# Half of the last block's centring moved from VectorE to TensorE, as a float32 product with a diagonal matrix

## The chip, the cores and the metric

The kernel runs on one core of a Trainium2 chip. A core has TensorE (matrix products into PSUM), VectorE, ScalarE and GpSimd (elementwise work), and SyncE, which issues DMAs; GpSimd issues DMAs too. In the profile they are PE, DVE, ACT, POOL and SP. Each engine works through its own queue in order, and engines wait for each other by semaphores. The metric is the device time of one execution in microseconds (us); shorter is better.

## The reference

One layer of a streaming encoder over 1024 rows of 1024 columns, in float32. Six products of the input feed two branches (a gated linear recurrence and a multi-scale pooling), which are gated and merged; the merged rows go through `w_out`, are added to the input, and each row is normalized:

```python
y = jnp.einsum('bsd,de->bse', merged, w_out[l]) + b_out[l]
x = _layer_norm(DEEPNORM_ALPHA * x + y, ln_gain[l], ln_bias[l])

def _layer_norm(x, g, b):
    mu = jnp.mean(x, axis=-1, keepdims=True)
    var = jnp.mean(jnp.square(x - mu), axis=-1, keepdims=True)
    return (x - mu) * lax.rsqrt(var + LN_EPS) * g + b
```

The change concerns the last step alone: `(x - mu) * g`, then the division by the deviation, then `+ b`, for one block of 128 rows.

## The kernel before, in words

**Products.** Every large product is made of seven block products in place of eight (a Strassen scheme over 2 x 2 blocks), and every float32 operand is split into a rounded half (`h`) and a rest (`l`) of the type float32r, so that each product of 128x128 by 128x512 takes three passes: h by h, h by l, l by h. TensorE is busy nearly all the time.

**The end of the kernel.** The last product, merged by `w_out`, works on the rows in two halves: blocks 0 to 3 and blocks 4 to 7, of 128 rows each; tile `zt[s]` (in the profile `z`) holds block s, which starts as the biased input. `o_product` (line 1490) is 12 matmuls into a PSUM bank, and `o_add` (line 1449) adds a bank to half of the columns of a block. The loop over `O_STEPS` (line 1510) ends with blocks 0 to 3; the last loop (line 1534) makes blocks 4 to 7, each from two products: bank `oc`, subtracted from columns 512 to 1023, then bank `oe`, added to columns 0 to 511. For block 7 (`last`) the second product is made in two halves of 256 columns.

**The norm.** `o_norm(s)` (line 1463) follows. For blocks 0 to 6, VectorE makes the negative mean `nm` from sums that came with the additions, ScalarE squares the block (`sq`) with a running sum, and takes the root (`sd`); VectorE centres and multiplies by the scale in two halves (`y`), takes the reciprocal of `sd`, and ScalarE multiplies `y` by it. GpSimd then adds `y` to the rows of the output by a DMA that accumulates (`add_to`, line 672); the norm's bias had been written there before (line 1441). For block 7, VectorE takes the statistics of each 256 columns (`bn_stats`, `bn_aggr` into `mv`), ScalarE takes the root, VectorE centres and scales by the gain in two halves of 512 columns, takes the reciprocal, multiplies by it and adds the bias, again in two halves, and SyncE stores each half. `g_row` and `be_row` hold the gain and the bias on all partitions.

**What sets the order.** The code does not issue instructions; it adds tasks to a planner (`Plan`, line 162), which puts them in an order and then emits them. The planner steps through a time of its own with a cost for each task (lines 222 to 258): a GpSimd task takes 0.15 + 0.002 for each column, and is taken to be ready 0.1 later; a DMA from SP takes 0.07 and lands 1.9 later, and its bytes at 270 KB in a us more; a GpSimd DMA takes 1.05; a ScalarE copy 0.12 + 0.00083 for each column. When an engine is free, it starts, among the tasks whose operands are ready by that time, the one with the earliest due time. The due time is that of the tasks which use the result (what TensorE needs comes first), and 40 after TensorE's place in the program for tasks that nobody needs soon. TensorE and GpSimd are exceptions: their tasks keep the order of the program (line 217):

```python
t.chain = self.last.get(eng) if eng in ("PE", "POOL") or ... else None
```

On the chip, each engine then keeps the planned order, however late an operand comes.

Of the kernel before, what the change touches and what calls it, by code (L numbers as in the profile page):

```python
# [11 lines left out]
F32 = mybir.dt.float32  # L12
F32R = mybir.dt.float32r
AF = mybir.ActivationFunctionType
ALU = mybir.AluOpType

P = 128
S = 1024
# [390 lines left out]
def layer_kernel(ctx: ExitStack, tc: tile.TileContext, xq, x, w_in, par, wg, w_pool, wpa, wpb, w_out, rows, out):  # L409
    nc = Plan(tc)  # L410

    def pool(name, bufs, space=None):
        kw = {} if space is None else {"space": space}
        return Pool(ctx.enter_context(tc.tile_pool(name=name, bufs=bufs, **kw)), bufs, space is bass.MemoryType.DRAM)
# [9 lines left out]
    dram = pool("dram", 8, bass.MemoryType.DRAM)  # L424

    def xt(name, dt=F32R, shape=(P, 2, H)):
        return xpool.tile(list(shape), dt, tag="x", name=name)
# [7 lines left out]
    def kt(name, dt=F32):  # L435
        return kpool.tile([P, S], dt, tag="k", name=name)

    def et(name):
        return epool.tile([P, H], F32, tag="e", name=name)

    def bank(name):
        return psum.tile([P, H], F32, tag="ps", name=name)
# [4 lines left out]
    out = Ref(result, as_strided(Ref.base, [S, D], [D, 1]))  # L447
    HALF = [slice(0, H), slice(H, S)]
    V, A = nc.vector, nc.scalar
# [25 lines left out]
    KQ = 4  # L475
# [196 lines left out]
    def add_to(t, u):  # L672
        nc.gpsimd.dma_start(t, u, accum_op=ALU.add, max_dma_last_dim=2048)
# [174 lines left out]
    rcnt, ones = (const.tile([P, PAD], F32, name=n) for n in ("rcnt", "ones"))  # L848
# [63 lines left out]
    def b_pool(g):  # L912
# [15 lines left out]
        if g == 1:  # L928
# [5 lines left out]
    sp, m, nl, y, z, z2, acc = (const.tile([P, 8], F32, name=n)  # L934
                                for n in ("sp", "sp_m", "sp_nl", "sp_y", "sp_z", "sp_z2", "sp_acc"))
# [198 lines left out]
    g = Group("A0", w.out, X, *takes0)  # L1134
# [37 lines left out]
    due, pools, last, ends, W = {}, {}, [], [], {}  # L1172
# [6 lines left out]
    for i in range(1, len(order)):  # L1179
# [17 lines left out]
        if i > 1:  # L1197
            g = Group(f"{kind}{c}", W.pop(i), X, *takes)
# [124 lines left out]
    def o_sum4(p):  # L1323

        V.scalar_tensor_tensor(t2[p], t2[p], -1.0, sums[p, 1], ALU.mult, ALU.subtract)
# [43 lines left out]
    for i, (n, j) in enumerate(steps):  # L1369
# [7 lines left out]
        if j == 1:  # L1377
            a, c, m1, um = [[None] * KQ for _ in range(4)]
        X_, W_ = ([(hi_[:, k, :], lo_[:, k, :]) for hi_, lo_ in ops[i][o:o + 2] for k in range(2)] for o in (0, 2))
        for g in range(KQ):  # L1380
# [5 lines left out]
            for q in range(KQ):  # L1386
                sl = slice(q * P, (q + 1) * P)
# [43 lines left out]
    zt = {}  # L1431
# [3 lines left out]
    g_row, be_row = (xt(f"row{i}", F32, (P, S)) for i in (1, 2))  # L1435
# [3 lines left out]
    BY_DMA = (0, 1, 2, 3, 4, 5, 6)  # L1439
# [4 lines left out]
    nc.gpsimd.memset(eps, EPS)  # L1444
    stats = const.tile([P, 4, 6], F32, name="stats")
    last = NK - 1


    def o_add(s, e, ps, sign, first, final, sl=slice(0, H)):
        z = zt[s][:, e * H:(e + 1) * H][:, sl]  # L1450
        op = ALU.add if sign > 0 else ALU.subtract
        if final and s != last:
            V.scalar_tensor_tensor(z, z, ALPHA if first else 1.0, ps, ALU.mult, op, accum_out=acc[:, 2 * s + e:2 * s + e + 1])
        elif first:
            V.scalar_tensor_tensor(z, z, ALPHA, ps, ALU.mult, op)
        else:
            V.tensor_tensor(z, z, ps, op)
        if final and s == last:
            for k in (range(2) if sl == slice(0, H) else (sl.start // (H // 2),)):
                i = 2 * e + k  # L1460
                V.bn_stats(stats[:, i, :], zt[s][:, i * H // 2:(i + 1) * H // 2])

    def o_norm(s):
        sd = const.tile([P, 1], F32, name=f"sd{s}")
        sls = [slice(e * H, (e + 1) * H) for e in range(2)]
        if s == last:
            mv = const.tile([P, 2], F32, name=f"mv{s}")
            V.bn_aggr(mv, stats)
            A.activation(sd, mv[:, 1:2], AF.Sqrt, bias=eps)
            mean, op = mv[:, 0:1], ALU.subtract  # L1470
        else:
            nm, var = (const.tile([P, 1], F32, name=f"{n}{s}") for n in ("nm", "var"))
            V.tensor_scalar(nm, acc[:, 2 * s:2 * s + 1], acc[:, 2 * s + 1:2 * s + 2], -1.0 / D, ALU.add, ALU.mult)
            sq = kt(f"sq{s}")
            A.activation(sq, zt[s], AF.Square, bias=nm, accum_out=var)
            A.activation(sd, var, AF.Sqrt, bias=eps, scale=1.0 / D)
            mean, op = nm, ALU.add
        y = zt[s] if s == last else xt(f"y{s}", F32, (P, S))
        for sl in sls:
            V.scalar_tensor_tensor(y[:, sl], zt[s][:, sl], mean, g_row[:, sl], op, ALU.mult)  # L1480
        V.reciprocal(sd, sd)
        if s in BY_DMA:
            A.mul(y, y, sd)
            add_to(out[s * P:(s + 1) * P, :], y)
            return
        for sl in sls:
            V.scalar_tensor_tensor(y[:, sl], y[:, sl], sd, be_row[:, sl], ALU.mult, ALU.add)
            nc.sync.dma_start(out[s * P:(s + 1) * P, sl], y[:, sl])

    def o_product(ps, j, g, start, stop, sl=slice(0, H)):  # L1490
        for q in range(KQ):
            mh, ml = (t[:, q % 2, g * P:(g + 1) * P] for t in om[j][q // 2])
            wh, wl = (t[:, q % 2, sl] for t in ow[j][q // 2])
            for i, (l, r) in enumerate(((mh, wh), (mh, wl), (ml, wh))):
                nc.tensor.matmul(ps, l, r, start=start and q == 0 and i == 0, stop=stop and q == KQ - 1 and i == 2,
                                 skip_group_check=True)


    def operands(j):
        f, w = (xt, xt) if j == 2 else (kt, wt)  # L1500
        if j != 6:
            for p in range(2):
                load_wo(j, p, rt)
            for p in range(2):
                cast_wo(j, p, w)
        o_input(j, f)

    a, c = ([None] * KQ for _ in range(2))
    operands(6)
    for i, j in enumerate(O_STEPS[:5]):  # L1510
        if j == 6:
            for p in range(2):
                o_sum4(p)
        operands(O_STEPS[i + 2])
        for g in range(KQ):
            if j == 1:
                a[g] = bank(f"oa_{g}")
            elif j == 7:
                c[g] = bank(f"oc_{g}")
            ps = c[g] if j == 7 else a[g]  # L1520
            o_product(ps, j, g, j in (1, 7), j == 3)
            if j == 1:
                o_add(4 + g, 0, ps, 1, True, False)
            elif j == 6:
                o_add(4 + g, 1, ps, -1, True, False)
            elif j == 7:
                o_add(g, 1, ps, -1, True, False)
            elif j == 5:
                o_add(g, 1, ps, -1, False, True)
            else:  # L1530
                o_add(g, 0, ps, 1, True, True)
                o_norm(g)

    for g in range(KQ):
        o_product(c[g], 4, g, False, True)
        o_add(4 + g, 1, c[g], -1, False, True)
        pieces = (slice(0, H),) if g < KQ - 1 else (slice(0, H // 2), slice(H // 2, H))
        for sl in pieces:
            ps = bank(f"oe_{g}_{sl.start}")[:, 0:sl.stop - sl.start]
            o_product(ps, 2, g, True, True, sl)  # L1540
            o_add(4 + g, 0, ps, 1, False, True, sl)
        o_norm(4 + g)
    nc.emit()

# [53 lines left out]
```

## Time and profile before

| | us |
|---|---|
| median of 3 runs | 739.97 |
| lowest and highest of them | 739.44, 1909.23 |
| the profiled execution | 739.99 |
| span of the profiled execution | 738.2 |
| its TensorE, busy | 730.1 |
| last matmul of `oe` begins | 730.64 |
| first and second store of block 7 issued | 734.47, 735.13 |

The span runs from the first to the last instruction that the profiler saw; the time of an execution is 1.8 us longer. In the views, a row of the timeline has the start in us from the span's start, the length in us, the engine, the line (that of the planner's helper for all: L396), the operation, output<-inputs by the tiles' names, their shapes, and in brackets how long the engine had been idle and what ended that. DMA queue q0 holds what GpSimd issues, q1 what SyncE issues; "us to landing" is the time from the issue of a DMA until its completion is seen.

### The profile page before, as it was taken

What the parts mean: (1) busy time and instruction counts of PE and PEld (TensorE: products, weight loads), DVE (VectorE), ACT (ScalarE), POOL (GpSimd) and SP (SyncE); (2) the same over time, 40 slices, a digit from 0 to 9 for tenths busy, and PEclk for the clock granted to TensorE, in tenths of its full rate; (3) what the DMA queues carried; (4) which work ended last, traced back from release to release, by engine and by line L of the source; (5) the groups of instructions that cost most, each with busy time, mean ns of one, the idle gap of its engine ahead of it and who ended that gap; (6) DMA issues with size and microseconds to landing.
All of it is one profiled execution on the core that took longest, in us unless ns stands there. A gap on an engine that the chain in (4) does not pass through costs nothing.

```text
span 738.2 us, 8796 instructions
## 1 busy us (share of the span) xinstructions
PE 730.1 (99%) x3254; PEld 599.4 (81%) x3254; DVE 600.5 (81%) x741; ACT 459.6 (62%) x588; POOL 69.7 (9%) x119
## 2 busy tenths in 40 slices
PE   9999999999999999999999999999999999999996
PEld 7887888888887878788888888888888888888885
DVE  6998896969696878977986768879948886999676
ACT  6686969686877868688844445447553545325473
POOL 0071111111001111100011000100000000000021
PEclk9999999999999999999999999999999999999999
DMA  8247888678988989750386954999679996758757
GB/s 317 86 158 200 282 180 267 142 240 214 306 167 217 327 210 279 203 126 35 110 201 127 235 121 158 275 293 346 230 259 302 314 328 232 245 224 229 199 84 145
DMA packets 64227, 158.98 MB, mean 215 GB/s; under 512 B 4340, under 2 KB 8308, under 8 KB 64120
## 3 DMA queue, kind: packets, MB, share of 16 engines
q1 hardware_dynamic: 43784, 106.39, 41.6%
q0 software_dynamic: 20112, 51.91, 33.7%
q8 instruction: 25, 0.41, 0.2%
q10 hardware_dynamic: 288, 0.13, 0.1%
q14 instruction: 18, 0.15, 0.1%
HBM read 137.43 MB, written 77.07 MB: 291 GB/s over the span
## 4 chain that ended last, share of the span: by engine, by line
PE 99%; DVE 0%; DVEq 0%; issue 0%
PE a_A L396 11%; PE a_B L396 11%; PE a_G L396 11%; PE oa L396 6%; PE pa_b L396 6%; PE pa_a L396 6%; PE c_B L396 6%; PE c_A L396 6%; PE c_G L396 5%; PE ps_s L396 3%; PE oc L396 3%; PE pc_b L396 3%; PE pc_a L396 3%; PE ps_pool L396 3%; PE e_B L396 3%; PE e_A L396 3%
## 5 line engine op out<-in xcount | busy, mean ns | idle before, releaser
L396 ACT ACT_TABLE_LOAD x38 | 48.8, 1283 | 2.4 <-PEq L1590 1.6
L396 DVE SCALAR_TENSOR_TENSOR xc<-xp,par_sb,xc 128x1023 f32<-128x1023 f32 (+2 forms) x24 | 30.7, 1280 | 0.5
L396 DVE TENSOR_TENSOR i<-i,xc 128x1024 f32<-128x1024 f32 x8 | 9.8, 1224 | 25.5 <-ACT i L396 25.5
L396 PE MATMUL pa_a<-oh,oh 128*128 128x512 f32 x64 | 24.9, 389 | 0.0
L396 PE MATMUL pa_a<-ol,oh 128*128 128x512 f32 x64 | 24.9, 389 | 0.0
L396 PE MATMUL pa_a<-oh,ol 128*128 128x512 f32 x64 | 24.9, 389 | 0.0
L396 PE MATMUL pa_b<-oh,oh 128*128 128x512 f32 x64 | 24.9, 389 | 0.0
L396 PE MATMUL pa_b<-ol,oh 128*128 128x512 f32 x64 | 24.9, 389 | 0.0
L396 PE MATMUL pa_b<-oh,ol 128*128 128x512 f32 x64 | 24.9, 389 | 0.0
L396 ACT ACTIVATE zb<-zb,par_sb 128x1024 f32<-128x1024 f32 (+1 forms) x16 | 15.0, 939 | 13.3 <-DVE zb L396 13.2
L396 ACT ACTIVATE r<-ps_g,par_sb 64x512 f32<-64x512 f32 x32 | 21.9, 685 | 2.1 <-DVE rb_B L396 0.8
L396 ACT ACTIVATE i<-ps_g,par_sb 64x512 f32<-64x512 f32 x32 | 21.9, 685 | 1.9 <-DVE r L396 1.4
L396 PE MATMUL c_A<-x64h,wd_A 128*128 128x512 f32 x64 | 21.0, 389 | 0.0
L396 PE MATMUL c_B<-x64h,wd_B 128*128 128x512 f32 x64 | 21.0, 389 | 0.0
L396 POOL DMA_DIRECT2D out<-y x7 | 8.5, 1210 | 130.5 <-ACT sd L396 117.6
L396 PE MATMUL ps_pool<-mixh,wp 128*128 128x512 f32 x64 | 20.4, 389 | 0.0
L396 PE MATMUL e_A<-x,wah_A 128*128 128x512 f32 x64 | 19.7, 389 | 0.0
L396 PE MATMUL e_B<-x,wah_B 128*128 128x512 f32 x64 | 19.7, 389 | 0.0
L396 POOL COPY paced<-pace 128x1 f32<-128x1 f32 x17 | 6.8, 399 | 124.6 <-ACT pace L396 124.6
L396 PE MATMUL c_G<-x64h,wd_G 128*128 128x512 f32 x56 | 18.4, 389 | 0.0
L396 DVE TENSOR_TENSOR_SCAN r<-a,i 128x1024 f32<-128x1024 f32 x8 | 18.3, 2282 | 0.1
L396 PE MATMUL e_G<-x,wah_G 128*128 128x512 f32 x56 | 17.2, 389 | 0.0
(521 smaller groups left out, 2537.4 us busy)
## 6 DMA issues: line engine op xcount, KB each, us to landing
sg<-sg SPq DMA_DIRECT2D x16, 512.0 KB, 4.7
ra_A<-in_w_in SPq DMA_DIRECT2D x8, 512.0 KB, 7.0
rb_A<-in_w_in SPq DMA_DIRECT2D x8, 512.0 KB, 6.5
xb<-bias SPq DMA_DIRECT2D x4, 1024.0 KB, 11.6
ya<-r SPq DMA_DIRECT2D x8, 512.0 KB, 6.1
xb<-in_x POOLq DMA_DIRECT2D x4, 1024.0 KB, 9.8
ra_B<-in_w_in SPq DMA_DIRECT2D x8, 512.0 KB, 5.4
rb_B<-in_w_in SPq DMA_DIRECT2D x8, 512.0 KB, 6.2
```

The lines of the kernel that those rows point to most:

```text
L396: getattr(getattr(nc, t.op[0]), t.op[1])(*a, **k)
```

## The change

For block 7, columns 512 to 1023 (`two`) are no longer centred on VectorE. With g the gain, (x - mu) * g = x * g - mu * g. GpSimd makes x * g (`zg`), and TensorE adds two float32 products in one PSUM bank, `centred`: an identity matrix times `zg`, and a diagonal matrix with -mu of each row times the gain. Columns 0 to 511 (`one`) are centred on VectorE as before. The scaling then reads the first half from SBUF and the second from the bank.

The tile `eye` (128x512) holds three 128x128 matrices beside each other: ONE is the identity, MINUS its negative, DIAG the diagonal with -mu. ONE is made through DRAM: GpSimd clears the tile; SyncE writes 128x129 zeros of it to `eye_d`, writes 128 ones to the first column there, and reads the first 128 * 128 numbers back as rows of 128, so that the ones lie on the diagonal. ScalarE makes MINUS once, and DIAG from it when the mean is known, ahead of the root. All this stands in the program between the loop over `O_STEPS` and the last loop.

The stores of blocks 0 to 6 are now put on a list and issued by `stores.pop()()`: for blocks 0 to 3 at the same place as before, for blocks 4 to 6 in the next turn of the last loop, behind its first `o_add`; in the last turn `zg` stands ahead of block 6's store.

```diff
     stats = const.tile([P, 4, 6], F32, name="stats")
     last = NK - 1
+    stores = []
...
         if s == last:
             mv = const.tile([P, 2], F32, name=f"mv{s}")
             V.bn_aggr(mv, stats)
+            mean, op = mv[:, 0:1], ALU.subtract
+            one, two = sls
+            y = zt[s]
+            V.scalar_tensor_tensor(y[:, one], y[:, one], mean, g_row[:, one], op, ALU.mult)
+            A.mul(eye[:, DIAG], eye[:, MINUS], mean)
             A.activation(sd, mv[:, 1:2], AF.Sqrt, bias=eps)
-            mean, op = mv[:, 0:1], ALU.subtract
+            nc.tensor.matmul(centred, eye[:, DIAG], g_row[:, two], start=False, stop=True, skip_group_check=True)
+            V.reciprocal(sd, sd)
+            for sl, src_ in ((one, y[:, one]), (two, centred)):
+                V.scalar_tensor_tensor(y[:, sl], src_, sd, be_row[:, sl], ALU.mult, ALU.add)
+                nc.sync.dma_start(out[s * P:(s + 1) * P, sl], y[:, sl])
+            return
...
-        y = zt[s] if s == last else xt(f"y{s}", F32, (P, S))
+        y = xt(f"y{s}", F32, (P, S))
         for sl in sls:
             V.scalar_tensor_tensor(y[:, sl], zt[s][:, sl], mean, g_row[:, sl], op, ALU.mult)
         V.reciprocal(sd, sd)
-        if s in BY_DMA:
-            A.mul(y, y, sd)
-            add_to(out[s * P:(s + 1) * P, :], y)
-            return
-        for sl in sls:
-            V.scalar_tensor_tensor(y[:, sl], y[:, sl], sd, be_row[:, sl], ALU.mult, ALU.add)
-            nc.sync.dma_start(out[s * P:(s + 1) * P, sl], y[:, sl])
+        A.mul(y, y, sd)
+        stores.append(lambda: add_to(out[s * P:(s + 1) * P, :], y))
...
                 o_norm(g)
+                stores.pop()()
+
+    ONE, MINUS, DIAG = (slice(i * P, (i + 1) * P) for i in range(3))
+    eye, zg = et("eye"), et("zg")
+    eye_d = dram.tile([P, P + 1], F32, tag="eye", name="eye_d")
+    nc.gpsimd.memset(eye, 0.0)
+    nc.sync.dma_start(eye_d, eye[:, 0:P + 1])
+    nc.sync.dma_start(eye_d[:, 0:1], ones[:, 0:1])
+    nc.sync.dma_start(eye[:, ONE], eye_d.rearrange("a b -> (a b)")[0:P * P].rearrange("(p m) -> p m", m=P))
+    A.mul(eye[:, MINUS], eye[:, ONE], -1.0)
 
     for g in range(KQ):
         o_product(c[g], 4, g, False, True)
         o_add(4 + g, 1, c[g], -1, False, True)
+        if g == KQ - 1:
+            nc.gpsimd.tensor_tensor(zg, zt[last][:, HALF[1]], g_row[:, HALF[1]], ALU.mult)
+        if g:
+            stores.pop()()
         pieces = (slice(0, H),) if g < KQ - 1 else (slice(0, H // 2), slice(H // 2, H))
         for sl in pieces:
             ps = bank(f"oe_{g}_{sl.start}")[:, 0:sl.stop - sl.start]
             o_product(ps, 2, g, True, True, sl)
             o_add(4 + g, 0, ps, 1, False, True, sl)
+        if g == KQ - 1:
+            centred = bank("centred")
+            nc.tensor.matmul(centred, eye[:, ONE], zg, start=True, stop=False, skip_group_check=True)
         o_norm(4 + g)
     nc.emit()
```

## The prediction

> **What bounds the kernel now.** I read the page first, for the engine that carries the span, then the chain of waits over the last 40 us.
>
> ```profile
> PE 730.1 (99%) x3254; PEld 599.4 (81%) x3254; DVE 600.5 (81%) x741; ACT 459.6 (62%) x588; POOL 69.7 (9%) x119
> ...
> PE 99%; DVE 0%; DVEq 0%; issue 0%
> ```
>
> TensorE is the bound until its last product. The chain's last pieces (start, length, what):
>
> ```profile
> 722.61 2.72 PE oe L396 x12
> ...
> 728.05 2.88 PE oe L396 x24
> 730.93 0.02 issue
> 730.95 0.43 DVE z L396
> ...
> 731.41 0.44 DVE stats L396
> ...
> 731.87 0.27 DVE mv L396
> ...
> 732.17 1.42 DVE z L396 x2
> 733.58 0.09 DVE sd L396
> ...
> 733.69 0.75 DVE z L396
> 734.44 0.66 DVEq L1594
> ```
>
> From 730.95 on, VectorE alone carries the end: the last addition, the statistics, two centrings (1.42 us together where one takes 0.75, so the second costs some 0.66), the reciprocal, two scalings. Only this tail can get shorter; even all of its 4 us is 0.6% of the run. The other rows that matter are of block 6 and block 7 on VectorE, then on ScalarE:
>
> ```profile
> 728.01 0.16 DVE L396 RECIPROCAL sd<-sd 128x1 f32<-128x1 f32 x1 [0.25 <-ACT sd L396]
> 728.09 0.68 DVE L396 TENSOR_TENSOR z<-z,oc 128x512 f32<-128x512 f32 x1
> ...
> 729.97 0.43 DVE L396 BATCH_NORM_STATS2 stats<-z 128x6 f32<-128x256 f32 x1
> 730.95 0.42 DVE L396 TENSOR_TENSOR z<-z,oe 128x256 f32<-128x256 f32 x1 [0.55 <-PE oe L396]
> ```
>
> ```profile
> 722.77 1.15 ACT L396 ACTIVATE y<-y,sd 128x1024 f32<-128x1024 f32 x1 [0.23 <-DVE sd L396]
> 726.40 1.16 ACT L396 ACTIVATE sq<-z,nm 128x1024 f32<-128x1024 f32 x1 [2.48 <-DVE nm L396]
> ...
> 728.21 1.15 ACT L396 ACTIVATE y<-y,sd 128x1024 f32<-128x1024 f32 x1 [0.23 <-DVE sd L396]
> 732.17 0.29 ACT L396 ACTIVATE sd<-mv,eps 128x1 f32<-128x1 f32 x1 [2.81 <-DVE mv L396]
> ```
>
> The reciprocal of block 6 stands in VectorE's queue ahead of all of block 7 and waits for ScalarE; VectorE's only slack behind it is the 0.55 us before 730.95. So what holds ScalarE up before 726.40 by more than 0.55 us moves the end.
>
> **The gain meant.** One centring leaves VectorE: the first scaling starts where the second centring did, and the last store is issued 0.66 us sooner, if nothing else is late. Two things must be there in time. The reciprocal needs `sd`, which now stands behind the 128x128 scaling that makes DIAG (nearest row, ScalarE's 128x128 cast, 297 ns, below): 732.17 + 0.30 + 0.29 = 732.76, and the one centring ends about 732.83, so no wait. The second scaling needs `centred`: DIAG at 732.47, VectorE free for it at about 732.17 + 0.66 + 0.09 + 0.66 = 733.6, so the float32 product has 1.1 us. No float32 product stands in the trace. From below it is one pass, 2.72 / 12 = 0.23; the nearest row for full accuracy is this kernel's own split in three passes, 0.68; from above a whole group of twelve, 2.72, a wait of 1.6 that would turn the gain into a loss of 0.9. I take 0.68: no wait. The Trainium skill, FP8 and Floating Point Precision, section TensorE Precision Notes, speaks against it: true float32 costs four passes through the array. By that rule it is 0.91 us, still inside the 1.1, and the sum stays; no run here shows it. The other product (eye times zg) runs while VectorE takes the statistics.
>
> **What the change adds to the queues.** GpSimd's order is the program's. So the clearing of `eye` stands behind block 3's store, and zg between the stores of blocks 5 and 6.
>
> ```profile
> 716.86 1.21 POOL L396 DMA_DIRECT2D out<-y  x1 [1.74 <-ACT y L396]
> ...
> 724.32 1.20 POOL L396 DMA_DIRECT2D out<-y  x1 [3.49 <-ACT y L396]
> 729.72 1.21 POOL L396 DMA_DIRECT2D out<-y  x1 [4.20 <-ACT y L396]
> ```
>
> ```profile
> L396 POOL TENSOR_TENSOR sp_acc<-sp_acc,sp_z 128x8 f32<-128x8 f32 x9 | 5.1, 567 | 0.8
> ...
> L396 POOL MEMSET rcnt<- 128x1 f32 x16 | 0.6, 103 | 0.0
> ...
> L396 POOL MEMSET ones<- 128x16 f32 x1 | 0.1, 112 | 0.3 <-POOLq L1590 0.3
> ```
>
> ```profile
> L396 ACT CAST gh<-gr 128x128 fp32r<-128x128 f32 x8 | 2.4, 297 | 0.0
> ```
>
> Clearing: 9 ns more for 15 more columns, so 0.1 + 0.3 for 512; done at 718.07 + 0.4 = 718.5. zg: at least 0.57 (the 128x8 row); two VectorE passes, 1.5, is my upper end; I take 1.1. Then come three DMAs on SP, each waiting for the one before: 66 KB out, 128 single numbers out, 64 KB back. SP has nothing else to issue until the last stores, so nothing is queued behind them there; but ScalarE's MINUS waits for the third. What such a DMA takes, free and beside GpSimd's traffic:
>
> ```profile
> gr<-in_wg SPq DMA_DIRECT2D x1, 64.0 KB, 1.8
> ```
>
> ```profile
> DMA packets 346, 0.81 MB, mean 238 GB/s; under 512 B 12, under 2 KB 12, under 8 KB 346
> ## 3 DMA queue, kind: packets, MB, share of 16 engines
> q0 software_dynamic: 346, 0.81, 109.9%
> issues: line engine op xcount, KB each, median us to landing
> rb_B<-in_w_in SPq DMA_DIRECT2D x1, 512.0 KB, 6.9
> gr<-in_wg SPq DMA_DIRECT2D x1, 64.0 KB, 8.1
> ```
>
> The first is the stretch 41.5 to 42.5, with idle queues: 1.8 us. The second is 287.3 to 290.7, with GpSimd's queue full: SP's two loads had been issued, and in 3.4 us not one packet of theirs moved (only q0 has a row). And this is the stretch in which `eye` is made, 718.5 to 725.5:
>
> ```profile
> DMA  9999999998999999999999999999989989999952
> ...
> q0 software_dynamic: 704, 1.35, 108.5%
> ```
>
> It is full, until about 725.5. Bounds for each DMA: 1.8 and 8.1 us. A free SP transfer moves its first packet 0.8 us after issue (the last stores, below), so a full queue costs 3.4 - 0.8 = 2.6 more, and I take 4.4 for the first: 722.9. The second would meet the same, but the queue runs empty at about 725.6; it lands 1.0 later, 726.6. The third is free: 728.4.
>
> **Where ScalarE waits.** Where MINUS stands in ScalarE's queue is the planner's choice, by its own figures (they order, they are no times of the chip). In its list for the kernel before, block 3's store starts at 716.36, and block 5's scaling `y` can start at 725.15. The clearing follows at 716.36 + 1.05, and by the planner's formulas MINUS is ready 1.27 + 2.21 + 1.97 + 2.21 later, at 725.08, when ScalarE is free: MINUS goes just ahead of block 5's `y`. On the chip that `y` started at 722.77. It, and block 6's square, now stand behind a wait that ends at 728.4.
>
> The sum: MINUS to 728.7, `y` of block 5 1.05 more, so the square of block 6 at 729.8 instead of 726.40, 3.4 late. Block 6's reciprocal, and VectorE behind it, is 3.4 late; 0.55 of slack goes; the tail starts 2.85 late. Less the 0.66 gained, the stores are issued 2.2 late.
>
> ```profile
> 734.47 1.02 SPq L396 DMA_DIRECT2D out<-z  x2
> ```
>
> ```profile
> DMA  8350000003999999999999993000000000000000
> ...
> out<-z SPq DMA_DIRECT2D x2, 256.0 KB, 2.1
> ```
>
> ```profile
> out<-y POOLq DMA_DIRECT2D x1, 512.0 KB, 5.5
> ```
>
> Before, GpSimd's last store (issued 729.72, 5.5 to landing) moved its last packets at about 734.7 (the strip runs from 734.4, 0.095 us a digit), and the last two stores had the queues alone from 735.3 to 736.7; the second landed at 735.1 + 2.1 = 737.2, and the span ended 1.0 later. Now block 5's store leaves at 724.32 + 5.95 = 730.3; block 6's `y` is 3.4 late, zg ends at 732.2 + 1.1 = 733.3, and block 6's store leaves then, behind block 5's: its packets run to about 738.6, over the last two stores, issued at 736.6 and 737.3. Free they land at 739.4; wholly behind, 738.6 + 1.4 + 0.5 = 740.5. The middle, 740.0, is 2.8 after 737.2. The profiled execution took 739.99 (its span 738.2, and 1.8 around it; the median is 739.97), so **742.8**, and 742.2 to 743.4 for the two ends.
>
> **Rivals.** *The change does what it says* (`eye` by 725.0: three free DMAs give 718.5 + 5.5 = 724.0, and a `y` that is 1.5 us late reaches nobody). Then 0.66 less; zg still pushes block 6's store by 0.3, whose packets then run into the last two stores' for some 0.3: 739.6. For it: 1.8 us free. Against it: the full strip.
>
> *SP's packets get their turns.* With 59.8 us of packet time (109.9% of 16 engines over 3.4 us) a packet of q0 takes 0.17 us; 8 rows an engine would wait 8 x 0.17 = 1.4, so 3.2 for a DMA: 721.7, 724.9, and `eye` at about 726.9. The tail is then 1.35 late, less 0.66, plus 0.4 of mixing: 741.1. The Trainium skill, DMA: Bandwidth & Descriptors, section Queues, rings and completion order, has this rule: each engine goes round its queues by packets. The 3.4 us without a packet speak against it here.
>
> *Later still, plainly slower.* If MINUS falls behind block 5's `y` (0.07 decides in the plan), that store leaves on time, and its packets fill the queue for the third DMA: 726.6 + 4.4 = 731.0. The square of block 6 starts at 731.3, 4.9 late; 4.9 - 0.55 - 0.66 = 3.7, with 0.5 of mixing: 744.2. The second DMA, of single numbers, can bring the same by being slower than any row shows. To reach 2% (14.8 us) all three would have to take 8.1.
>
> **Numbers.** Forecast 0.50; as meant 0.17; turns 0.15; later 0.13; 0.05 for something else (the product as the last wait among it, about 740.5). The range 739.6 to 745.0 leaves out some of the gains and of the latest cases. What a measurement of this kernel can tell is about 2%; every case but the 8.1 one is within it: faster 0.01, same 0.98, slower 0.01.
>
> **What would show it.** Right: the trace after has MINUS on ScalarE between block 5's `sd` and `y`, idle until a DMA into `eye` at about 728; a reciprocal of block 6 that waits for `sd` some 3 us; one centring of 128x512 at the end, and a scaling from `centred` that doesn't wait. Wrong: `eye` there before 725.5 (the DMAs weren't held), `y` of block 5 at 722.8 (the order was another), or a wait for `centred`.

## The result and the profile after

| | before | after |
|---|---|---|
| median, us | 739.9 | 743.77 (742.74 to 744.44, 6 runs) |
| ratio of the times | | 1.0052, 95% interval 1.0042 to 1.0063 |
| the profiled execution | 739.99 | 743.75 |
| its span | 738.2 | 742.0 |
| `mv` of block 7 known | 732.13 | 735.00 |
| second store of block 7 issued | 735.13 | 738.37 |

The change costs 3.9 us, half a per cent: reliably more than nothing, and far within 2%. One of the six executions before took 1909.23 us, and the ratio leaves it out. The forecast was 742.8 with a range from 739.6 to 745.0.

ScalarE's timeline after the change, at the place where MINUS was expected:

```profile
721.86 0.29 ACT L396 ACTIVATE sd<-var,eps 128x1 f32<-128x1 f32 x1
728.77 0.31 ACT L396 ACTIVATE eye<-eye 128x128 f32<-128x128 f32 x1 [6.61 <-DMA eye<-eye_d]
728.98 1.14 ACT L396 ACTIVATE y<-y,sd 128x1024 f32<-128x1024 f32 x1
730.02 1.13 ACT L396 ACTIVATE sq<-z,nm 128x1024 f32<-128x1024 f32 x1
...
735.04 0.40 ACT L396 ACTIVATE eye<-eye,mv 128x128 f32<-128x128 f32 x1 [2.09 <-DVE mv L396]
```

MINUS stands between `sd` and `y` of block 5 and idles ScalarE for 6.61 us; the square of block 6 starts at 730.02 (726.40 before). What it does to VectorE:

```profile
731.61 0.16 DVE L396 RECIPROCAL sd<-sd 128x1 f32<-128x1 f32 x1 [4.22 <-ACT sd L396]
731.69 0.67 DVE L396 TENSOR_TENSOR z<-z,oc 128x512 f32<-128x512 f32 x1
...
734.74 0.26 DVE L396 BATCH_NORM_AGGREGATE mv<-stats 128x2 f32<-128x24 f32 x1
735.04 0.75 DVE L396 SCALAR_TENSOR_TENSOR z<-z,mv,row 128x512 f32<-128x512 f32 x1
735.71 0.15 DVE L396 RECIPROCAL sd<-sd 128x1 f32<-128x1 f32 x1
735.90 0.75 DVE L396 SCALAR_TENSOR_TENSOR z<-z,sd,row 128x512 f32<-128x512 f32 x1
737.59 0.75 DVE L396 SCALAR_TENSOR_TENSOR z<-centred,sd,row 128x512 f32<-128x512 f32 x1 [0.94 <-PE centred L396]
```

The reciprocal of block 6 comes 3.60 later than before, and all of block 7 behind it. One centring is left, as meant; the second scaling waits 0.94 for the product, which it was not to do. TensorE shows why, in its timeline and then in three stretches (the columns of the second are length, busy time of PE, PEld, DVE, ACT and POOL, granted clock, DMA share, GB/s):

```profile
730.26 0.28 PE L396 MATMUL oe<-wo2h,o2l 128*128 128x256 f32 x1
733.77 2.03 PE L396 MATMUL centred<-zg,eye 128*128 128x512 f32 x2 [3.23 <-POOL zg L396]
735.59 1.90 PE L396 MATMUL centred<-row,eye 128*128 128x512 f32 x2
```

```profile
728.00:731.00 3.00, 2.54 (x22) 2.33 (x20) 0.00 (x0) 2.23 (x3) 0.48 (x1) 1.00 0.07 19
731.00:734.00 3.00, 0.23 (x1) 0.24 (x2) 2.32 (x7) 1.69 (x4) 2.25 (x3) 0.97 0.62 70
734.00:737.30 3.30, 3.30 (x4) 0.72 (x4) 2.51 (x6) 0.58 (x2) 0.87 (x1) 0.51 1.10 178
```

A float32 product is two matmuls. TensorE had stood without work for 3.23 us, its granted clock is 0.51 in the last stretch, and there the product on the path takes 1.90 us. GpSimd's queue and the transfers into `eye`:

```profile
717.08 1.19 POOL L396 DMA_DIRECT2D out<-y  x1 [1.76 <-ACT y L396]
717.80 1.01 POOL L396 MEMSET eye<- 128x512 f32 x1
...
730.52 1.18 POOL L396 DMA_DIRECT2D out<-y  x1 [9.49 <-ACT y L396]
732.45 1.26 POOL L396 TENSOR_TENSOR zg<-z,row 128x512 f32<-128x512 f32 x1 [0.75 <-DVE z L396]
733.67 1.21 POOL L396 DMA_DIRECT2D out<-y  x1
```

```profile
eye_d<-eye SPq DMA_DIRECT2D x1, 64.5 KB, 5.6
eye<-eye_d SPq DMA_DIRECT2D x1, 64.0 KB, 1.7
eye_d<-ones SPq DMA_DIRECT2D x1, 0.5 KB, 2.6
```

The transfers follow each other from 718.84 to 728.66. The page sums its chain of waits over the whole span, so TensorE's products before the end hide this; the same chain, cut to the end of the span, shows where its last stretch starts (start, length, what):

```profile
687.66 10.00 DMA wor<-in_w_out
...
704.33 1.25 ACT sq L396 x2
...
717.80 1.01 POOL eye L396
...
721.03 9.47 issue
...
732.45 1.27 POOL zg L396
...
733.77 3.73 PE centred L396 x4
```

It begins with a load of `w_out` that lands at 697.66 and runs through the norms of blocks 0 to 3 to the clearing. From there it stays in GpSimd's queue; its 9.47 of "issue" is the time in which block 5's store waits for ScalarE's `y` (GpSimd's rows above), which stands behind MINUS and so behind `eye`. In the kernel before, the chain is TensorE's products up to 730.93, and none of this set the end.

The 3.74 us that the span grew are, from these rows: `mv` later by 2.87; from `mv` to the issue of the second store 3.37 instead of 3.00, so +0.37; from there to the end of SP's wait for the landing (740.63, before 737.19) 2.26 instead of 2.06, so +0.20; and from there to the end 1.33 instead of 1.03, so +0.30.

### The profile page after: what moved, and what is told of

Read it like the earlier page. It is cut to its first block, busy times and chain, and to the rows that moved or that the text cites. A ratio compares the mean times of both kernels' runs of the same rounds, so it can differ in the third digit from the quotient of the medians.

```text
span 742.0 us, 8817 instructions
## 1 busy us (share of the span) xinstructions
PE 733.5 (99%) x3258; PEld 601.1 (81%) x3258; DVE 599.8 (81%) x740; ACT 459.9 (62%) x590; POOL 71.2 (10%) x121
## 4 chain that ended last, share of the span: by engine, by line
PE 93%; issue 2%; ACT 2%; DMA 1%; DVE 1%; POOL 1%; POOLq 0%; ACTq 0%; DVEq 0%
PE a_A L396 11%; PE a_B L396 11%; PE a_G L396 10%; PE pa_b L396 6%; PE pa_a L396 6%; PE c_B L396 6%; PE c_A L396 6%; PE c_G L396 5%; PE ps_s L396 3%; PE oa L396 3%; PE pc_b L396 3%; PE pc_a L396 3%; PE ps_pool L396 3%; PE e_B L396 3%; PE e_A L396 3%; PE e_G L396 3%
```

## The experiments

Each is compared with the kernel before on the same chip (739.83 in the first group of four, 739.66 in the second of four, 739.49 in the last of three).

**The transfers early.** The eight lines that make `eye` are put ahead of the loop over `O_STEPS`; `nc.not_until(698.0)` keeps the planner from starting them before that time of its own.

```diff
+    with nc.not_until(698.0):
+        ONE, MINUS, DIAG = (slice(i * P, (i + 1) * P) for i in range(3))
...
+        A.mul(eye[:, MINUS], eye[:, ONE], -1.0)
     a, c = ([None] * KQ for _ in range(2))
```

> The changed kernel, with the making of `eye` (clearing, three DMAs, MINUS) moved ahead of the first output product, when GpSimd stores nothing yet. Theory (the loss is ScalarE's wait for `eye`): block 6's square starts at about 726.4 again, the mean of block 7 is known at about 732.1, 2.9 us sooner than in the changed kernel; the wait for `centred` of some 0.9 us stays, so that the second store leaves about 0.4 later than in the kernel before: 740.3 us. Rival (the float32 products, zg and the moved stores cost the time): it stays above 742.5. Second rival (without the hold the gain is as meant): 739.3.

740.17 us, ratio 1.0003 (0.9994 to 1.0012). The 3.9 us are gone, and the 0.66 that the change was to bring doesn't show either. Its timelines on VectorE and TensorE:

```profile
732.58 0.75 DVE L396 SCALAR_TENSOR_TENSOR z<-z,sd,row 128x512 f32<-128x512 f32 x1
733.40 0.75 DVE L396 SCALAR_TENSOR_TENSOR z<-centred,sd,row 128x512 f32<-128x512 f32 x1
```

```profile
730.30 1.02 PE L396 MATMUL centred<-zg,eye 128*128 128x512 f32 x2
732.17 1.13 PE L396 MATMUL centred<-row,eye 128*128 128x512 f32 x2 [0.84 <-ACT eye L396]
```

TensorE has had no long pause, the same product takes 1.13 us, and VectorE waits under 0.1. A wait of 0.9 that stays was expected, so that the time comes near the 740.3 expected is luck. The second store is issued 2.50 after `mv` instead of 3.00: VectorE does its part. The last packet moves 4.64 after `mv` instead of 4.71: the transfers give it back. And from the end of SP's wait for the landing to the end of the span it takes 1.33 instead of 1.03 (see **The exit** below).

**MINUS alone moved.** `eye` stays late, but MINUS is pushed behind block 6's `y` in ScalarE's queue.

```diff
-    A.mul(eye[:, MINUS], eye[:, ONE], -1.0)
+    with nc.not_until(732.0):
+        A.mul(eye[:, MINUS], eye[:, ONE], -1.0)
```

> The changed kernel, with MINUS alone put behind block 6's `y` on ScalarE; the clearing and the three DMAs stay where they are. Theory: nothing waits behind MINUS any more, so block 5's `y` starts at about 722.8 and its store at 724.3, whose packets hold the third DMA until some 731; MINUS is made by 731.5, still ahead of the mean at 732.1: 740.3 us, as with `eye` made early. Rival (the DMAs themselves, or their share of the queues, cost the time): above 742.

740.30, ratio 1.0008 (0.9999 to 1.0017); one of the eleven executions took 742.67, and it was not profiled. ScalarE's row:

```profile
730.14 0.31 ACT L396 ACTIVATE eye<-eye 128x128 f32<-128x128 f32 x1 [0.98 <-DMA eye<-eye_d]
```

`eye` lands even later than in the changed kernel, at 730.04, and it costs nothing, since only DIAG waits behind MINUS now. So the loss is one instruction's place in ScalarE's queue.

**The transfers alone.** The kernel before, with the lines that make `eye`, which nothing uses: products and zg are left out, and block 7 is centred on VectorE.

> The kernel before, with the making of `eye` added where the change has it (clearing, three DMAs, MINUS), and nothing that uses it: the norm is that of the kernel before. Theory: ScalarE waits some 6.6 us ahead of block 5's `y`, the mean of block 7 is known 2.9 late, and all of it shows: 742.8 to 743.3 us. Rival (the loss is in the products): 739.9.

744.68, ratio 1.0063 (1.0051 to 1.0076): more than was expected, and no less than with the products (the intervals overlap). The chain of its profiled execution, 745.31, says why it is late by more:

```profile
688.23 11.28 DMA wor<-in_w_out
...
720.74 5.38 DMA eye_d<-eye
...
730.43 0.07 ACT eye L396
```

There the load of `w_out` landed at 699.51 instead of 697.66, and everything down to `eye` came 1.7 later. So the loss needs neither products nor zg, and in these two profiles its size hangs on a load that the kernel before hides.

**One pass in place of float32.** `eye` early, and the products' operands rounded to float32r, so that each is one matmul.

```diff
+            A.mul(eye_r[:, P:2 * P], eye[:, MINUS], mean)
...
+            nc.tensor.matmul(centred, eye_r[:, P:2 * P], g_r, start=False, stop=True, skip_group_check=True)
```

> `eye` made early, as in the first of these runs, and both products in one pass of float32r in place of float32 (operands rounded to float32r: zg by GpSimd, the others by ScalarE), so that the centring of half of block 7 is less exact. Theory (the float32 product on the path, 1.9 us long, is what eats the 0.66 us): VectorE no longer waits for `centred`, both stores leave 0.66 sooner than in the kernel before: 739.3 us, 0.9 below the run with float32. Rival (the wait is in the hand-over from ScalarE to TensorE to VectorE, not in the passes): no more than 0.2 below it.

739.88, ratio 1.0001 (0.9993 to 1.0010). Half of the forecast failed: the product takes 0.50 instead of 1.13 and the scaling doesn't wait, but of the 0.9 us expected 0.3 came, which the intervals don't tell from nothing. The 0.9 was a wait that the kernel with early `eye` no longer had; its second store went from 2.50 to 2.34 after `mv`.

**TensorE kept busy.** The changed kernel, with 14 products into the bank of `centred` before the first one that counts.

```diff
             centred = bank("centred")
+            for _ in range(14):
+                nc.tensor.matmul(centred, om[2][0][0][:, 0, 0:P], ow[2][0][0][:, 0, 0:H], start=True, stop=True, skip_group_check=True)
```

> The changed kernel with 14 extra products (128x512, split operands already in memory, 0.23 us each, into the bank of `centred`, overwritten by the next product) on TensorE between its last `oe` and the product of `eye` and zg, so that it isn't idle from 730.5 to 733.8. Both theories expect the granted clock to stay at 1.0, the float32 products to take 1.12 us instead of 1.90, and the second scaling to wait 0.1 us instead of 0.94, so that the second store is issued some 0.85 us sooner. Theory 'the end is set by block 6's store': its packets run to about 739.0 and the last two stores' 512 KB need another 1.4 us behind them, as in the first experiment, so the time falls by 0.1 to 0.4 only: 743.4 to 743.7. Rival 'the halved clock is on the path': the whole 0.85 us comes off, 742.9.

742.87, ratio 1.0044 (1.0032 to 1.0057): by the number the rival's case. But in its profile `eye` landed 1.1 sooner than in the changed kernel's, and from block 6's reciprocal to the last landing it took 9.1 us and the changed kernel 9.0. (The second scaling still waited 0.41, since the product with zg stood behind the extra ones until 734.01.) The two had been measured at different times, so they were run side by side:

> The changed kernel as it is, beside the next kernel on the same chip, because the kernel with the warm TensorE came out at 742.87 and the changed one, measured on another occasion, at 743.77. The profiles put that difference on `eye`, which landed 1.1 us sooner in the one than in the other because block 3's store left 0.8 us sooner, and not on the clock: from block 6's reciprocal to the last landing both took 9.0 us. Theory 'block 6's store sets the end, and the transfers into `eye` vary': this and the next agree within 0.4 us, at 742.9 to 743.9. Rival 'the halved clock is on the path': this is 0.7 to 0.9 above the next.

> The kernel with the 14 extra products again, for the comparison with the one before. Theory: within 0.4 us of it. Rival 'the halved clock is on the path': 0.7 to 0.9 below it.

The changed kernel 742.06, ratio 1.0036 (1.0024 to 1.0049); with TensorE kept busy 743.04, 1.0045 (1.0032 to 1.0057). The one at half clock is not the slower one. They were expected within 0.4 us of each other and are 0.98 apart, the other way round from the rival's forecast; in the profiled executions, 742.69 and 743.39, `eye` landed 0.70 apart, as the table below shows. The second scaling, without the extra products and with them:

```profile
736.55 0.75 DVE L396 SCALAR_TENSOR_TENSOR z<-centred,sd,row 128x512 f32<-128x512 f32 x1 [1.03 <-PE centred L396]
```

```profile
736.30 0.75 DVE L396 SCALAR_TENSOR_TENSOR z<-centred,sd,row 128x512 f32<-128x512 f32 x1
```

And the products on TensorE, again without and with:

```profile
734.37 2.08 PE L396 MATMUL centred<-row,eye 128*128 128x512 f32 x2 [0.60 <-ACT eye L396]
```

```profile
730.38 3.36 PE L396 MATMUL centred<-wo2h,o2h 128*128 128x512 f32 x14
733.58 1.02 PE L396 MATMUL centred<-zg,eye 128*128 128x512 f32 x2
735.07 1.13 PE L396 MATMUL centred<-row,eye 128*128 128x512 f32 x2 [0.47 <-ACT eye L396]
```

The second store is issued 3.45 after `mv` without, 2.50 with; SP's wait for its landing ends 5.70 and 5.68 after `mv`. A gain of 0.95 us on VectorE is worth nothing, because the last packet comes 1.41 and 1.29 after the last one of GpSimd's queue, whenever SP's stores were issued. That queue is emptied by block 6's store. The chain of the changed kernel in this run begins elsewhere than in the first:

```profile
686.92 16.33 PE oa L396 x72
...
717.88 5.34 DMA eye_d<-eye
...
727.64 0.07 ACT eye L396
```

Here the load landed at 696.70 and no longer stands in the chain, which starts from TensorE's products. Four profiles that go on alike from block 3's store:

| | load landed | block 3's store | `eye` landed | reciprocal of block 6 | span |
|---|---|---|---|---|---|
| changed kernel, second time | 696.70, not in the chain | 716.12 | 727.53 | 730.48 | 740.9 |
| TensorE kept busy, second time | 697.39 | 716.80 | 728.23 | 731.17 | 741.6 |
| changed kernel | 697.66 | 717.08 | 728.66 | 731.61 | 742.0 |
| transfers alone | 699.51 | 718.96 | 730.33 | 733.27 | 743.5 |

The span follows `eye` nearly us for us. That accounts for the difference between the two profiled executions of the changed kernel, 742.69 and 743.75; the medians, 742.06 and 743.77, lie further apart, and no profile says why.

What `eye` itself follows shows when its transfers are set beside GpSimd's stores. In all seven profiles with `eye` made late, the first transfer, issued behind block 3's store, lands within 0.2 us of that store (724.40 and 724.59 in the changed kernel), and the next one 0.2 us after block 4's (726.98 and 726.79). Why they land together was not tried.

**One transfer more.** The changed kernel, with the 128 single numbers written twice.

```diff
     nc.sync.dma_start(eye_d[:, 0:1], ones[:, 0:1])
+    nc.sync.dma_start(eye_d[:, 0:1], ones[:, 1:2])
```

> The changed kernel with a fourth chained transfer on SP, of the same 128 single numbers, ahead of the one that brings `eye` back (1.4 us where it was seen on free queues). Theory 'ScalarE's wait for `eye` sets the end': every us that `eye` comes later is a us at the end; the queue of GpSimd is empty by then, so +1.4 to +1.8: 745.2 to 745.6. Rival 'the loss is in GpSimd's order or in the products at the end': `eye` has slack, 743.8.

745.24, ratio 1.0072 (1.0059 to 1.0084): the size expected, but not the same case, and the profiled execution was the shortest of the five, 743.64, so it doesn't show the median's 745.24. ScalarE in that profile:

```profile
729.95 0.31 ACT L396 ACTIVATE eye<-eye 128x128 f32<-128x128 f32 x1 [6.75 <-DMA eye<-eye_d]
730.17 1.13 ACT L396 ACTIVATE sq<-z,nm 128x1024 f32<-128x1024 f32 x1
```

The planner now put MINUS behind block 5's `y`, in front of block 6's square: the prediction's case "later still". Block 5's store then left at 723.61, and the third transfer took 3.56 us beside its packets. So this run bears out the order of ScalarE's queue, but not a price for each us that `eye` comes later.

**Block 6's store ahead of zg**, in the kernel with early `eye` and one-pass products.

```diff
-        if g == KQ - 1:
-            nc.gpsimd.tensor_tensor(zg, zt[last][:, HALF[1]], g_row[:, HALF[1]], ALU.mult)
         if g:
             stores.pop()()
+        if g == KQ - 1:
+            nc.gpsimd.tensor_tensor(zg, zt[last][:, HALF[1]], g_row[:, HALF[1]], ALU.mult)
```

> The experiment before with `eye` made early and one-pass products (739.88), with block 6's store ahead of zg in GpSimd's queue. zg is then ready at about 731.8, its product ends at 732.3, the one with DIAG at 732.8, still ahead of the second scaling at 733.3. Theory 'what the change gains on VectorE is lost in the transfers, because zg pushes block 6's store by 0.4 us into the last two stores': the second store is issued 2.4 us after mv and takes 2.1 to land as before, not 2.6: 739.4. Rival 'the last transfers don't depend on block 6's store': 739.9. Rival 'zg behind the store is too late and VectorE waits': 740.3 or more.

739.49, ratio 0.9998 (0.9989 to 1.0007): 0.4 below the kernel it was made from in the medians, as expected, but 0.2 when each is set against the kernel before on its own chip (+0.05 and -0.17), and the intervals of the two overlap. The last stores' rows, with zg first (the one-pass kernel) and with the store first:

```profile
out<-z SPq DMA_DIRECT2D x2, 256.0 KB, 2.6
```

```profile
out<-z SPq DMA_DIRECT2D x2, 256.0 KB, 2.0
```

The landing is back at 2.0 (2.1 in the kernel before), and SP's wait for the last one ends 4.42 after `mv` instead of 4.96.

**The exit.** In all these kernels SyncE, after its last store, waits in turn for the eight semaphores of its DMAs, which are given out in rotation. The sequencer's rows of the trace show each step to take 0.06 us. Before, the last store has the sixth semaphore of the eight; three transfers more make it the first. The same kernel as the last, with one of the three issued by GpSimd, so that the last store has the eighth:

```diff
-        nc.sync.dma_start(eye_d[:, 0:1], ones[:, 0:1])
+        nc.gpsimd.dma_start(eye_d[:, 0:1], ones[:, 0:1])
```

> The one before, with the transfer of 128 single numbers into `eye_d` issued by GpSimd instead of SP. SP then has one transfer less, and its last store gets the last of the eight semaphores that SP waits for in turn at the end, instead of the first: seven waits of 0.06 us that stood behind the last landing stand ahead of it. Theory 'the order of these waits is worth 0.4 us': 739.0. Rival 'they are hidden by other engines' ends': the same as the one before, 739.4. As another transfer stands in GpSimd's queue, its stores of the first blocks may move, which have slack.

739.04, ratio 0.9991 (0.9983 to 1.0000). From the end of the wait for the last landing to the drain that follows these waits, 0.49 us became 0.06 (736.59 to 737.08, and 736.11 to 736.17); in the kernel before it is 0.19 (737.19 to 737.38). The same again beside the last group:

> The kernel with `eye` made early, one-pass products, block 6's store ahead of zg and the last store's semaphore at the end of the exit list, again, to say whether it beats the kernel before: 0.5 to 0.9 us below it (0.66 from the centring, 0.12 from the exit, less what the transfers give back), 739.0. Rival 'its first measurement was luck': no difference from the kernel before.

739.04, ratio 0.9992 (0.9983 to 1.0001). That is 0.62 and 0.45 us below the kernel before; the two intervals end at 1.0000 and 1.0001, so it stands at the edge of what can be told. Some 0.12 of it is the exit, which has nothing to do with centring.

## Why the prediction was right

- **The clearing behind block 3's store**: right. It ended at 718.81 (718.5 forecast). It took 1.01 and not 0.4, since the small rows of GpSimd were too far from 512 columns; that it began at 717.80, before the row of block 3's store ended at 718.27, made up for half of this.
- **Three transfers through a full queue**: right in sum, `eye` at 728.66 (728.4), with two sizes that were off: the first took 5.6 (4.4), the second 2.6 (3.7), the third 1.7 (1.8). The first's error did no harm, because the sum took the second's landing from the moment when GpSimd's queue runs empty, 726.6 (it was 726.98), whenever the first had landed. Of the first, this is the stretch 718 to 722:

```profile
q0 software_dynamic: 399, 0.78, 110.3%
q1 hardware_dynamic: 28, 0.01, 1.8%
```

SP's packets did move here, 28 of them beside 399. The Trainium skill (DMA: Bandwidth & Descriptors, section Queues, rings and completion order) has every DMA engine go round its queues by packets. By the prediction's turns that would have been 3.2 us for the first transfer. It took 5.6, so the turns, if they are taken, are far from equal.
- **The planner's place for MINUS**: right, between `sd` and `y` of block 5. The case with one transfer more shows how near the other place was.
- **The wait's way to VectorE**: right. The square of block 6 at 730.02 (729.8), `mv` 2.87 late (2.85). Making the transfers alone brings the whole loss, and moving MINUS alone takes it back to within noise of the kernel before.
- **The gain of 0.66 with no wait for `centred`**: wrong, in the size of the product. 0.68 was taken for it; it is 1.02 to 1.13 at full clock and 1.90 to 2.08 at half, and VectorE waited 0.94. That TensorE would stand idle for 3.2 us before it, and be granted half its clock, was not thought of. A wait for `centred` is one of the signs that the prediction had named against itself. The Trainium skill (FP8 and Floating Point Precision, section TensorE Precision Notes) has four passes for true float32, 0.91 us as the prediction worked it out; that is nearer to the 1.02 to 1.13 at full clock, though the trace shows two matmuls and not four.
- **The last transfers**: the mechanism was there, the size was off. The middle between free and "wholly behind block 6's store" was taken, 740.0; the wait for the last landing ended at 740.63, beyond the upper end of 740.5. So the 0.66 less on VectorE counts for nothing in this kernel: SP's last stores end 1.3 to 1.4 us after GpSimd's queue is empty, with the second of them issued 2.50 or 3.45 after `mv`. The extra 0.94 of waiting cost nothing for the same reason.
- **The exit**: +0.30. The sum took the way from the last landing to the end as unchanged.

Forecast +2.8, measured +3.8 in the profiled execution: 0.6 in the last transfers, 0.3 in the exit, the rest rounding. The rival *as meant* would not have been 739.6 either: with `eye` early it is 740.17, which is 0.34 above the kernel before and not 0.4 below it.

How much later `eye` comes in a given run hangs, in three of the four profiles above, on the load of `w_out`; what makes that load land at 696.7 or 699.5 was not tried.

## What to carry to other kernels

When a change adds a small preparation off the critical path, look at which instruction of a busy queue first waits for it, and at what stands behind that: here a 0.3 us scaling with no hurry stood ahead of the norm of block 6, and moving it alone took the loss back to within noise. Before shortening the last engine's work, see what moves in the DMA queues at that moment: if another queue's transfer ends after the issue of the last store, the end is that transfer's, and up to 0.95 us gained ahead of it changed nothing. A chain that did not set the end in the old profile brings its own variation with it when the change makes it the critical one.

## What the runs showed of the hardware

- A float32 product of 128x128 by 128x512 is two matmuls in the trace: 1.02 to 1.13 us at a granted clock of 1.0, 1.90 to 2.08 at 0.5; one float32r pass took 0.50.
- TensorE's granted clock was 0.5 from 733.85 to 737.26 in the changed kernel, after 3.2 us without work, while 14 extra products kept it at 1.0. The pause is no fixed figure: measured again, the clock fell at 734.22, 0.5 us after a product that had itself run at 1.0, and in the kernel before only 5.1 us after the last matmul (730.92 and 736.03).
- Writing 64.5 KB took SP 5.6 us beside a full GpSimd queue, and writing 128 single numbers 2.6 (1.4 where GpSimd stored nothing, with `eye` early); reading the 64 KB back on free queues took 1.7.
- Small SP transfers landed with GpSimd's stores: the first within 0.2 us of the store issued before it, the second 0.2 us behind the next, in seven profiles of seven.
- Where the last store's semaphore stands in SyncE's list at the end is worth up to 0.43 us.
